# Stationary tokens for the mixer's output projection, turned back by VectorE and DMA, and the first two MLP blocks side by side

## The chip, the cores and the metric

The program runs on one core of a Trainium2 chip. The metric is device time in microseconds (us), the median of the runs. Engines in the profile: PE is TensorE (PEld its weight loads), DVE is VectorE, ACT is ScalarE, POOL is GpSimd, SP is SyncE; a name with q (SPq, ACTq) is that engine's sequencer, where it issues transfers.

## The reference, cut to what matters

One layer on 16 meta tokens and 256 tokens of width 2048, all in float32:

```python
h = h + hybrid_mixer(rmsnorm(h, norm_mix_g), ...)
h = h + squared_relu_mlp(rmsnorm(h, norm_mlp_g), w_ff1, w_ff2)
return rmsnorm(h, final_norm_g)[:, N_META:]

# the end of hybrid_mixer
y = sigmoid(gate_fox) * (o_fox @ w_o_fox) + sigmoid(gate_gla) * (o_gla @ w_o_gla)
return y @ w_out                               # 256 x 2048 times 2048 x 2048

def squared_relu_mlp(xn, w1, w2):              # 2048 -> 8192 -> 2048
    return jnp.square(jax.nn.relu(xn @ w1)) @ w2
```

The part ahead of `y` (projections, forgetting attention, gated linear attention) is left as it was.

## The kernel before, in words

**Products.** Each float32 operand is held as two fp32r parts, high and low, and a product is three matmuls: high by high, high by low, low by high. All weights stream once from HBM in the order of `stream()`, in loads of 512 KB (`raw`, five buffers, issued by SyncE in order). ScalarE copies the high part into a buffer `w` (L133, L177) and VectorE subtracts to get the low part (L134, L178). There are five buffers `w` of one 128x1024 tile pair each, so ScalarE can be five tiles ahead of TensorE and no more.

**Two forms.** `gemm2` keeps a weight tile stationary and streams the tokens (L191: 512 columns, both parts of 256 tokens; L192: 256 columns). Its result has features on partitions, as the residual stream `h` has, 128 output features at a time. `token_rows` keeps 128 tokens stationary and streams 512 weight columns (L224 to L226, twice for 256 tokens). Its result has tokens on partitions, 512 features at a time, and must be turned. A block below is 512 output features; its 16 contraction steps come in four quarters, each one call of `wide_weights` with two tiles `w`.

**A turn.** `turn` transposes 32x32 squares on VectorE (L237), sends the tile to DRAM in four transfers (L244, `there<-turn`) and fetches it back (L248, `turn<-there`), all issued by ScalarE. The list `behind` sets when: each call of `wide_weights` or `next_weights` counts the entries down, and an entry falls due behind the copy of the call's last tile. Slots 5, 6 and 7 are the send, the fetch and the use (`then`).

**Order of the work around the change.** `columns(b)` makes blocks 1, 2 and 3 of `y` in token form and turns them; block 0 is then made by `gemm2` in two pairs of features (`j0` 0 and 2). `y` is split in two parts (L282, L283). The output projection is 16 times `gemm2` over `y`; each result is added to `h`, scaled by the MLP's norm gain into the two parts of `x2`, and its squares are summed in `acc2`. The MLP runs in four groups `g` of 2048 hidden features: ff1 as token blocks (`hidden`: ReLU times `r2` and square on ScalarE, turn, two parts of `a`), then ff2 (`gathered`), which in groups 0 to 2 adds up in token form. In group 0 `norm2` runs inside the first block: four matmuls over `acc2` (L1017), then the root `r2` on VectorE. `spread` (L1024, L1027) sends `r2` through DRAM and broadcasts it into `r2b` on SyncE's queue, between the weight loads. The last group makes two ff1 blocks in token form and the features 8 to 15 with `gemm2`, and its ff2 with `gemm2`. At the end `finish` scales by the last norm and stores.

Tile's scheduler sets each engine's order from a model of the timeline; each engine then works through its order, and a wait holds what stands behind it on that engine.

Of the kernel before, what the change touches and what calls it, by code (L numbers as in the profile page):

```python
# [16 lines left out]
P = 128  # L17
D = 2048
KT = D // P
# [20 lines left out]
def stream():  # L40
# [12 lines left out]
    for j in range(2):  # L53
        s += [("in", O_GF + 128 * j, 0), ("in", O_GG + 128 * j, 0)]
    s += [("in", O_GF + 128 * 2, 0)]
    for b in range(1, 4):
        s += [("in", o + 128 * j, 0) for o in (O_GF, O_GG) for j in range(4 * b, 4 * b + 4)]
        s += [("fox", 128 * j, 0) for j in range(4 * b, 4 * b + 4, 2)]
        s += [("gla", 128 * j, 0) for j in range(4 * b, 4 * b + 4)]
    for j in (0, 2):  # L60
        if j:
            s += [("in", o, 0) for o in (O_GG + 128 * 2, O_GF + 128 * 3, O_GG + 128 * 3)]
        s += [("fox", 128 * j, 0)]
        s += [("gla", 128 * j, 0), ("gla", 128 * (j + 1), 0)]
# [8 lines left out]
def trunk(ctx: ExitStack, tc: tile.TileContext, hT, w_small, w_all, consts, w_alpha2, out):  # L73
# [141 lines left out]
    def token_rows(x, n, between=None, nk=KT, **kw):  # L215

        pts = [[bank(px, "pt") for _ in range(2)] for _ in range(n)]
        for i, q in [(i, q) for i in range(n) for q in range(nk // 4 - 1)] + [(i, nk // 4 - 1) for i in range(n)]:
            w = wide_weights(chunk[0] + 4 * i, q, **kw)
            for k in range(4 * q, 4 * q + 4):  # L220
                hi, lo = w(k)
                for t, ps in enumerate(pts[i]):
                    xh, xl = (x[:, k, o, P * t : P * t + P] for o in range(2))
                    nc.tensor.matmul(steps(ps), xh, steps(hi), start=(k == 0), stop=False)  # L224
                    nc.tensor.matmul(steps(ps), xh, steps(lo), start=False, stop=False)  # L225
                    nc.tensor.matmul(steps(ps), xl, steps(hi), start=False, stop=(k == nk - 1))  # L226
                if between and k == 9:
                    between()
# [4 lines left out]
    def turn(rows, then, both, into=None):  # L233
# [13 lines left out]
        behind.append([5, away])  # L247
        behind.append([6, lambda: nc.scalar.dma_start(back, there)])  # L248
        behind.append([7, lambda: then(back.rearrange("p (c t j r) -> p j t c r", c=4, t=2, r=32))])
# [747 lines left out]
    for j in range(KT):  # L997
        add_residual(j, gemm2(next_weights(), y))
        nc.scalar.activation(x2[:, j, 0, :], ht[:, j, :], AF.Identity, scale=gain(1, j))
        nc.vector.scalar_tensor_tensor(x2[:, j, 1, :], ht[:, j, :], gain(1, j),  # L1000
                                       x2[:, j, 0, :].bitcast(F32), op0=ALU.mult, op1=ALU.subtract)
        square_sum(j, acc2)
# [4 lines left out]
    nc.gpsimd.memset(unit.bitcast(F32), 1.0)  # L1007

# [27 lines left out]
    def turn_tile():  # L1036
        return gat.tile([P, KT * P], F32, tag="o", name=nm("turn"))

    def hidden(a, b, pt):
# [8 lines left out]
        turn([lambda t=t: part(t) for t in range(2)], lambda back: turned_parts(a, b, back), turn_tile())  # L1048
# [3 lines left out]
    def gathered(g, b, pt):  # L1052
# [10 lines left out]
        def add(back):  # L1063
            for j in range(4 * b, 4 * b + 4):
                r = ht[:, j, :].rearrange("p (t c r) -> p t c r", t=2, r=32)
                nc.gpsimd.tensor_tensor(r, r, back[:, j - 4 * b], op=ALU.add)
# [10 lines left out]
    for g in range(NG):  # L1077
# [3 lines left out]
        for b in range(2 if g == NG - 1 else 4):  # L1081
            hidden(a, b, *token_rows(x2, 1, norm2 if (g, b) == (0, 0) else None))
# [3 lines left out]
    for f in range(8, KT):  # L1086
# [74 lines left out]
    def finish(i):  # L1161
# [92 lines left out]
```

## Time and profile before

| What | Value |
|---|---|
| Median of 3 runs (lowest to highest) | 1529.1 us (1528.81 to 1529.36) |
| The profiled execution: time, span | 1529.71 us, 1528.0 us |
| Mean granted TensorE clock | 0.998 |
| Busy PE, DVE, ACT, POOL | 99%, 63%, 51%, 9% of the span |
| HBM read, written | 300.46 MB, 13.12 MB (205 GB/s over the span) |
| Output projection, first matmul to the MLP's first | 752.41 to 838.99 us |
| ff1 of group 0, first matmul to the first of its ff2 | 838.99 to 924.4 us |
| Landing of a weight load, a send, a fetch (median) | 4.0, 4.4, 5.1 us |
| Landing of `line<-r`, of `r2b<-line` (median) | 8.7, 6.9 us |

A row of the order of time gives start, duration, engine, line, operation, output<-input, shapes and count, and in brackets the idle time of the engine before it with what ended it. A row with a count above one is merged, from the first start to the last end. Waits read: engine and line, what was waited for, total us, times, longest.

### The profile page before, as it was taken

How to read it: one execution, taken by the hardware profiler on the slowest of the kernel's cores; microseconds unless marked ns; L12 is line 12 of the kernel's file. 1: busy time of each engine (PE TensorE's matmuls, PEld its weight loads, DVE VectorE, ACT ScalarE, POOL GpSimd, SP SyncE). 2: the span in 40 equal slices, each digit the busy share in tenths (PEclk: the TensorE clock that was granted, in tenths of full speed). 3: DMA queues.
4: the chain of work that ended last, by engine and by line, in shares of the span. 5: the costliest groups of instructions: out<-in, count | busy, mean ns of one | idle time of the engine just before them, and what ended most of it. 6: DMA issues, size and time to landing. Idle time of an engine off the chain costs nothing.

```text
span 1528.0 us, 22647 instructions
## 1 busy us (share of the span) xinstructions
PE 1516.4 (99%) x8646; PEld 1354.7 (89%) x8646; DVE 969.2 (63%) x1355; ACT 781.9 (51%) x1138; POOL 131.1 (9%) x206
## 2 busy tenths in 40 slices
PE   9999999999999999999999999999999999999997
PEld 8999999999998888888899888888888888888997
DVE  7898858586665454546787565445555455656765
ACT  7766444455555434344556455445544455345663
POOL 5012010121101000000011000000000000220012
PEclk9999999999999999999999999999999999999999
DMA  9545555565555667666566587667775677787652
GB/s 321 172 149 182 178 163 186 161 213 169 170 172 181 201 203 223 212 213 210 198 204 199 173 282 253 200 198 238 243 232 195 219 249 245 235 268 246 205 188 103
DMA packets 215472, 315.07 MB, mean 206 GB/s; under 512 B 12170, under 2 KB 180116, under 8 KB 215236
## 3 DMA queue, kind: packets, MB, share of 16 engines
q1 hardware_dynamic: 199636, 289.76, 58.6%
q10 hardware_dynamic: 15552, 22.75, 4.3%
q8 instruction: 68, 1.11, 0.3%
q0 software_dynamic: 176, 1.12, 0.2%
q14 instruction: 40, 0.33, 0.1%
HBM read 300.46 MB, written 13.12 MB: 205 GB/s over the span
## 4 chain that ended last, share of the span: by engine, by line
PE 95%; DVE 2%; ACT 1%; issue 1%; DMA 0%; SPq 0%; POOL 0%; POOLq 0%; DVEq 0%; ACTq 0%
PE ps L191 17%; PE pt L226 17%; PE pt L225 17%; PE pt L224 17%; PE ps L192 9%; PE psa L196 4%; PE psa L200 4%; PE psa L198 4%; PE ps L455 1%; PE ps L1120 1%; PE ps L457 1%; DVE w L134 1%; PE ps L1102 0%; DMA raw<-w_all_dram 0%; PE pa L653 0%
## 5 line engine op out<-in xcount | busy, mean ns | idle before, releaser
L178 DVE TENSOR_TENSOR w<-raw,w 128x1024 fp32r<-128x1024 f32 x292 | 359.6, 1233 | 342.2 <-ACT w L177 330.0
L177 ACT CAST w<-raw 128x1024 fp32r<-128x1024 f32 x292 | 305.1, 1046 | 368.7 <-PE pt L226 353.5
L134 DVE TENSOR_TENSOR w<-raw,w 128x1024 fp32r<-128x1024 f32 x230 | 282.9, 1230 | 109.9 <-ACT w L133 106.8
L133 ACT CAST w<-raw 128x1024 fp32r<-128x1024 f32 x230 | 240.9, 1049 | 101.9 <-PE ps L192 32.2
L226 PE MATMUL pt<-w,x 128*128 128x512 f32 x640 | 243.2, 380 | 0.0
L225 PE MATMUL pt<-w,x 128*128 128x512 f32 x640 | 243.2, 380 | 0.0
L224 PE MATMUL pt<-w,x 128*128 128x512 f32 x640 | 243.2, 380 | 0.0
L191 PE MATMUL ps<-x,w 128*128 128x512 f32 x671 | 227.4, 383 | 0.0
L192 PE MATMUL ps<-x,w 128*128 128x256 f32 x671 | 184.1, 274 | 0.0
L196 PE MATMUL psa<-x,w 128*128 128x272 f32 x640 | 181.7, 285 | 0.0
L200 PE MATMUL psa<-x,w 128*128 128x272 f32 x640 | 179.7, 282 | 0.0
L198 PE MATMUL psa<-x,w 128*128 128x272 f32 x624 | 175.9, 282 | 0.0
L224 PE MATMUL pt<-w,a 128*128 128x512 f32 x384 | 145.9, 380 | 0.0
L225 PE MATMUL pt<-w,a 128*128 128x512 f32 x384 | 145.9, 380 | 0.0
L226 PE MATMUL pt<-w,a 128*128 128x512 f32 x384 | 145.9, 380 | 0.0
L191 PEld LDWEIGHTS ps<-x,w 128*128 128x128 f32 x671 | 126.0, 188 | 21.4
L226 PEld LDWEIGHTS pt<-w,x 128*128 128x128 f32 x640 | 120.1, 188 | 20.7
L224 PEld LDWEIGHTS pt<-w,x 128*128 128x128 f32 x640 | 120.1, 188 | 20.7
L225 PEld LDWEIGHTS pt<-w,x 128*128 128x128 f32 x640 | 120.1, 188 | 20.6
L192 PEld LDWEIGHTS ps<-x,w 128*128 128x128 f32 x671 | 126.0, 188 | 0.0
L196 PEld LDWEIGHTS psa<-x,w 128*128 128x128 f32 x640 | 120.2, 188 | 0.2
L200 PEld LDWEIGHTS psa<-x,w 128*128 128x128 f32 x640 | 120.2, 188 | 0.1
(343 smaller groups left out, 2179.7 us busy)
## 6 DMA issues: line engine op xcount, KB each, us to landing
raw<-w_all_dram SPq DMA_DIRECT2D x525, 512.0 KB, 4.0
there<-turn ACTq DMA_DIRECT2D x72, 128.0 KB, 4.4
turn<-there ACTq DMA_DIRECT2D x18, 512.0 KB, 5.1
raw<-w_all_dram SPq DMA_DIRECT2D x26, 256.0 KB, 3.4
raw<-w_all_dram SPq DMA_DIRECT2D x8, 384.0 KB, 6.7
h<-hT_dram SPq DMA_DIRECT2D x8, 275.0 KB, 6.7
there<-sg ACTq DMA_DIRECT2D x12, 128.0 KB, 4.5
yf<-there ACTq DMA_DIRECT2D x3, 512.0 KB, 4.1
```

Source lines behind the costliest of these rows:

```text
L133: copied = nc.scalar.copy(hi[:, k, :], r).ins
L134: nc.vector.tensor_tensor(lo[:, k, :], r, hi[:, k, :].bitcast(F32), op=ALU.subtract)
L177: copied = nc.scalar.copy(hi, r).ins
L178: nc.vector.tensor_tensor(lo, r, hi.bitcast(F32), op=ALU.subtract)
L191: nc.tensor.matmul(steps(ps), hi, steps(row(x)), start=first, stop=False)
L192: nc.tensor.matmul(steps(ps[:, 0:NT]), lo, steps(x[:, 0, :]), start=False, stop=last)
L196: nc.tensor.matmul(steps(ps[:, X_LO]), hi, steps(x_lo[:, k]), start=first, stop=False, skip_group_check=True)
L198: nc.tensor.matmul(steps(ps[:, 0:NA]), lo, steps(x_hi[:, k]), start=False, stop=last and hi is None, skip_group_check=True)
L200: nc.tensor.matmul(steps(ps[:, 0:NA]), hi, steps(x_hi[:, k]), start=False, stop=last, skip_group_check=True)
L224: nc.tensor.matmul(steps(ps), xh, steps(hi), start=(k == 0), stop=False)
L225: nc.tensor.matmul(steps(ps), xh, steps(lo), start=False, stop=False)
L226: nc.tensor.matmul(steps(ps), xl, steps(hi), start=False, stop=(k == nk - 1))
```

## The change

The output projection uses `token_rows` over `y`, four blocks, each turned (`mixed`); the residual sum, `x2` and the squares follow behind the turn. `y`'s blocks 0 to 2 are now the ones made in token form, and block 3 the one by `gemm2`, so that the last made is the last read. In group 0 the first two ff1 blocks are one call of `token_rows`: three quarters of the first, three of the second, then the last quarter of each, with `norm2` behind step 13 of the first; both are turned at the same slots. The last group makes a third ff1 block in token form. Two smaller edits: the residual sum behind a turned ff2 block takes two wide operations on GpSimd in place of four, and `finish` joins two stores.

```diff
-    for b in range(1, 4):
+    for b in range(3):
         s += [("in", o + 128 * j, 0) for o in (O_GF, O_GG) for j in range(4 * b, 4 * b + 4)]
...
-                if between and k == 9:
+                if between and (i, k) == (0, 13):
                     between()
...
-    def turn(rows, then, both, into=None):
+    def turn(rows, then, both, into=None, slot=5):
...
-        behind.append([5, away])
-        behind.append([6, lambda: nc.scalar.dma_start(back, there)])
-        behind.append([7, lambda: then(back.rearrange("p (c t j r) -> p j t c r", c=4, t=2, r=32))])
+        behind.append([slot, away])
+        behind.append([slot + 1, lambda: nc.scalar.dma_start(back, there)])
+        behind.append([slot + 2, lambda: then(back.rearrange("p (c t j r) -> p j t c r", c=4, t=2, r=32))])
...
-    for b in range(1, 4):
+    for b in range(3):
         columns(b)
-    for j0 in (0, 2):
-        gates = ahead[0:4] if j0 == 0 else [ahead[4]] + [gate() for _ in range(3)]
+    for j0 in (12, 14):
+        gates = ahead[0:4] if j0 == 12 else [ahead[4]] + [gate() for _ in range(3)]
...
-    y = operand(keep, "y", at=16, tag="s1")
+    y = operand(keep, "y", at=48, tag="s1")
...
-    for j in range(4):
+    for j in range(12, KT):
         split_to(y[:, j, 0, :], y[:, j, 1, :], yf[:, j, :])
...
-    for j in range(KT):
-        add_residual(j, gemm2(next_weights(), y))
-        nc.scalar.activation(x2[:, j, 0, :], ht[:, j, :], AF.Identity, scale=gain(1, j))
-        nc.vector.scalar_tensor_tensor(x2[:, j, 1, :], ht[:, j, :], gain(1, j),
-                                       x2[:, j, 0, :].bitcast(F32), op0=ALU.mult, op1=ALU.subtract)
-        square_sum(j, acc2)
+    def mixed(b, pt):
+        def add(back):
+            for t in range(2):
+                r = ht[:, 4 * b : 4 * b + 4, P * t : P * t + P].rearrange("p j (c r) -> p j c r", r=32)
+                nc.vector.tensor_tensor(r, r, back[:, :, t], op=ALU.add)
+            for j in range(4 * b, 4 * b + 4):
+                nc.scalar.activation(x2[:, j, 0, :], ht[:, j, :], AF.Identity, scale=gain(1, j))
+                nc.vector.scalar_tensor_tensor(x2[:, j, 1, :], ht[:, j, :], gain(1, j),
+                                               x2[:, j, 0, :].bitcast(F32), op0=ALU.mult, op1=ALU.subtract)
+                square_sum(j, acc2)
+        turn([lambda ps=ps: ps for ps in pt], add, turn_tile(), slot=4 if b == 3 else 5)
...
+    for b in range(4):
+        mixed(b, *token_rows(y, 1))
...
         def add(back):
-            for j in range(4 * b, 4 * b + 4):
-                r = ht[:, j, :].rearrange("p (t c r) -> p t c r", t=2, r=32)
-                nc.gpsimd.tensor_tensor(r, r, back[:, j - 4 * b], op=ALU.add)
+            for t in range(2):
+                r = ht[:, 4 * b : 4 * b + 4, P * t : P * t + P].rearrange("p j (c r) -> p j c r", r=32)
+                nc.gpsimd.tensor_tensor(r, r, back[:, :, t], op=ALU.add)
...
-        for b in range(2 if g == NG - 1 else 4):
-            hidden(a, b, *token_rows(x2, 1, norm2 if (g, b) == (0, 0) else None))
+        for b0, n in ((0, 2), (2, 1), (3, 1)) if g == 0 else [(b, 1) for b in range(3 if g == NG - 1 else 4)]:
+            for b, pt in enumerate(token_rows(x2, n, norm2 if n == 2 else None), b0):
+                hidden(a, b, pt, 3 if (g, b) == (NG - 1, 2) else 5)
...
-    for f in range(8, KT):
+    for f in range(12, KT):
         relu2(a, f, gemm2(next_weights(low=True), x2))
...
-                store(nc.sync, j0, 4)
+                if j0 == 0:
+                    store(nc.sync, j0, 4)
                 scale(eng, j0 + 4, 4, r)
-                store(nc.sync, j0 + 4, 4)
+                store(nc.sync, j0 + 4 if j0 == 0 else j0, 4 if j0 == 0 else 8)
```

The change moves instructions at two places that the prediction speaks of. Lines of the changed kernel stand up to two lower than those of the kernel before up to the output projection (L177 is L175, L244 is L242, L248 is L246), and some nine higher in the MLP (L1044 is L1053, L1027 is L1039).

First, ScalarE in ff1 of group 0. Before, behind the copies for the first quarter of the third block, it stands so; `turn_8824` is the first block's turned tile, `u_8970` the second block's rows:

```order
L177 CAST w_8982<-raw_8981 128x1024
L177 CAST w_8987<-raw_8986 128x1024
L244 DMA there_8831<-turn_8824 32x4x256 x4
L177 CAST w_9020<-raw_9019 128x1024
L177 CAST w_9025<-raw_9024 128x1024
L248 DMA turn_8824<-there_8831 128x1024
L1044 ACTIVATE u_8970<-pt_8832,r_8653 128x512
L1044 ACTIVATE u_8970<-pt_8833,r_8653 128x512
L177 CAST w_9055<-raw_9054 128x1024
L1045 ACTIVATE u_8970<-u_8970 128x512 x2
L177 CAST w_9060<-raw_9059 128x1024
L282 CAST a_8660<-turn_8824 128x4x128 x2
```

Now, behind the copies `w_8973` and `w_8978` for the first quarter of the fourth block, it stands so; `turn_8806` and `turn_8815` are the first and the second block's tiles, `u_8961` the third block's rows:

```order
L242 DMA there_8813<-turn_8806 32x4x256 x4
L242 DMA there_8822<-turn_8815 32x4x256 x4
L175 CAST w_9015<-raw_9014 128x1024
L175 CAST w_9020<-raw_9019 128x1024
L246 DMA turn_8806<-there_8813 128x1024
L246 DMA turn_8815<-there_8822 128x1024
L1053 ACTIVATE u_8961<-pt_8823,r_7823 128x512
L1053 ACTIVATE u_8961<-pt_8824,r_7823 128x512
L175 CAST w_9051<-raw_9050 128x1024
L1054 ACTIVATE u_8961<-u_8961 128x512 x2
L175 CAST w_9056<-raw_9055 128x1024
L280 CAST a_8450<-turn_8806 128x4x128 x2
```

Sends, fetches and casts of two tiles stand together where those of one stood; the cast of `turn_8815` is the next row, ahead of the next weight copies. Counted in tiles `w` from the MLP's first (tile 0), `w_8973`, `w_8978`, `w_9015`, `w_9020`, `w_9051` and `w_9056` are tiles 24 to 29.

Second, SyncE's queue around `spread`. Before, `raw_8936` and `raw_8941` are the loads for tiles 14 and 15 of the MLP, `line` holds `r2` in DRAM:

```order
L175 DMA raw_8936<-w_all_dram 128x4x256
L175 DMA raw_8941<-w_all_dram 128x4x256
L1024 DMA line<-r_8653 128x1 x2
L175 DMA raw_8981<-w_all_dram 128x4x256
L1027 DMA r2b<-line 128x64 x4
L175 DMA raw_8986<-w_all_dram 128x4x256
```

Now `raw_8927` and `raw_8932` are the loads for tiles 22 and 23:

```order
L173 DMA raw_8927<-w_all_dram 128x4x256
L173 DMA raw_8932<-w_all_dram 128x4x256
L1036 DMA line<-r_7823 128x1 x2
L1039 DMA r2b<-line 128x64 x3
L173 DMA raw_8972<-w_all_dram 128x4x256
L1039 DMA r2b<-line 128x64
L173 DMA raw_8977<-w_all_dram 128x4x256
```

The store of `r2` and its broadcasts come eight tiles later, and no weight load stands between the store and the first broadcast any more.

More of the change, by code (lines that the diff above doesn't have):

```diff
@@ L1034, in relu2, with hidden @@
         split_to(a[:, f, 0, :], a[:, f, 1, :], s)
-    def turn_tile():
-        return gat.tile([P, KT * P], F32, tag="o", name=nm("turn"))
-    def hidden(a, b, pt):
+    def hidden(a, b, pt, slot):
         u = gat.tile([P, 2, 512], F32, tag="u", name=nm("u"), bufs=1)
@@ L1046, in part @@
             return u[:, t, :]
-        turn([lambda t=t: part(t) for t in range(2)], lambda back: turned_parts(a, b, back), turn_tile())
+        turn([lambda t=t: part(t) for t in range(2)], lambda back: turned_parts(a, b, back), turn_tile(), slot=slot)
     rows = gat.tile([P, 2, D], F32, name="rows", bufs=1)
```

12 lines of the change are left out of this document (6 added, 6 removed).

## The prediction

> **What bounds it now.** I read the page first, its busy table and its chain, then PE's waits after the mixer's attention, then the order of time around the places of the change.
>
> ```profile
> PE 1516.4 (99%) x8646; PEld 1354.7 (89%) x8646; DVE 969.2 (63%) x1355; ACT 781.9 (51%) x1138; POOL 131.1 (9%) x206
> PE 95%; DVE 2%; ACT 1%; issue 1%; DMA 0%; SPq 0%; POOL 0%; POOLq 0%; DVEq 0%; ACTq 0%
> PE ps L192 <- DVE w L134: 0.5, 1, 0.5
> PE pn L1146 <- ACT sq L1127: 0.3, 1, 0.3
> ```
>
> TensorE is the bound: 99% busy, 95% of the chain. From 560 us on it waits 0.8 us that the profile can name, so a term must shorten its stream or open a hole in it. "Busy" overlaps neighbours, so I take pitches, from start to start, at the seam between output projection (L191/L192, stationary weights) and MLP (L224 to L226, stationary tokens).
>
> ```profile
> 757.99 0.38 PE L191 MATMUL ps<-y,w 128*128 128x512 f32 x1
> 838.66 0.38 PE L191 MATMUL ps<-y,w 128*128 128x512 f32 x1
> 838.88 0.27 PE L192 MATMUL ps<-y,w 128*128 128x256 f32 x1
> 838.99 0.38 PE L224 MATMUL pt<-w,x 128*128 128x512 f32 x1
> 839.21 0.38 PE L225 MATMUL pt<-w,x 128*128 128x512 f32 x1
> 847.79 0.38 PE L225 MATMUL pt<-w,x 128*128 128x512 f32 x1
> ```
>
> 757.99 is the projection's 14th contraction step and 838.66 its 256th: 80.67 us over 242 steps is 0.3333 us for one step of 128 output columns. 839.21 to 847.79 is 39 matmuls of 512 columns: 0.2200 us each.
>
> **The change, part by part.** *Stationary tokens.* Four projection blocks and one block of the last ff1 change form. A block of 512 output columns took 64 x 0.3333 = 21.33 us; now it is 96 x 0.2200 = 21.12. Five blocks give 5 x 0.213 = **1.07 us**. Both forms stream the same number of columns; the gain is only that fewer, longer matmuls carry it. The Trainium skill (TensorE: Matmul & The Clock Gate, section Back-to-back issue gap) gives a warm matmul of N columns N / 2.4 + 2.5 ns: 215.7 and 109.2 ns, an estimate of 0.43 us for the five blocks. The rows show 220.0 and 113.3 ns, a larger fixed part, so the trace differs and its 1.07 stands.
>
> *y's order.* Before, the blocks finished last in feature layout are y's steps 0 to 3, and the projection starts on them.
>
> ```profile
> 752.41 0.38 PE L191 MATMUL ps<-y,w 128*128 128x512 f32 x1
> 755.30 0.38 PE L192 MATMUL ps<-y,w 128*128 128x256 f32 x1 [0.50 <-DVE w L134]
> 755.62 0.41 ACT L282 CAST y<-yf 128x256 fp32r<-128x256 f32 x1 [1.63 <-DVE yf L967]
> 756.06 0.43 DVE L283 TENSOR_TENSOR y<-yf,y 128x256 fp32r<-128x256 f32 x1 [0.47 <-ACT y L282]
> 756.54 0.50 PE L191 MATMUL ps<-y,w 128*128 128x512 f32 x1
> ```
>
> From the projection's first matmul to the MLP's first are 838.99 - 752.41 = 86.58 us, where 256 x 0.3333 = 85.33 are work: **1.25 us** is lost, all in these rows. The scheduler starts other outputs early, but y's fourth block is ready only at 756.49. After, these are steps 14 and 15, first read 14 x 6 x 0.22 = 18.5 us into the projection and ready 4.1 us into it. The stall goes whole (between 0 and 1.25 I take 1.25); next late is nothing for 14 us.
>
> *The way back from the projection.* Its rows now need two transposes, four sends, one fetch, the residual sum and the two parts of x2. One such turn of the MLP shows the pace:
>
> ```profile
> L224 PE MATMUL pt<-w,a x384: 380/380/380, 924.4 to 1346.1; 128*128 128x512 f32 x192
> 922.07 0.34 ACTq L248 DMA_DIRECT2D turn<-there  x1
> 923.89 1.35 ACT L1044 ACTIVATE u<-pt,r 128x512 f32<-128x512 f32 x2 [0.94 <-PE pt L226]
> 926.07 1.15 ACT L1045 ACTIVATE u<-u 128x512 f32<-128x512 f32 x2
> 928.89 1.14 ACT L282 CAST a<-turn 128x512 fp32r<-128x512 f32 x2 [0.65 <-DMA turn<-there]
> 927.35 1.30 DVE L237 STREAM_TRANSPOSE turn<-u 128x512 f32<-128x512 f32 x2
> 929.67 1.29 DVE L283 TENSOR_TENSOR a<-turn,a 128x512 fp32r<-128x512 f32 x2
> 841.74 0.96 DVE L1000 SCALAR_TENSOR_TENSOR x<-h,x 128x256 fp32r<-128x256 f32 x1
> ```
>
> Consumer at 924.4, turned data usable at 928.9. By the same slots x2's third block is fetched 4.5 us into the MLP. The adds (1.29), one weight subtraction (1.23) and four scalings (at most 0.96 each) end by 4.5 + 1.3 + 1.2 + 3.8 = 10.8; its steps start at 10.6, 11.9, 13.2 and 14.5, and the first is ready at 8.0. Hidden, with 2.6 us of cover. The fourth block has its slots one earlier and is first read after six quarters (31.7 us), since the two MLP blocks leave their last quarters to the end: hidden. If a cover goes, each us missing costs one. I price them 0.
>
> *norm2 and r2.* Rows of the root and of what SyncE does with it:
>
> ```profile
> 852.19 1.04 PE L1017 MATMUL pn<-unit,parts 128*128 128x512 f32 x4
> 856.99 1.23 DVE L178 TENSOR_TENSOR w<-raw,w 128x1024 fp32r<-128x1024 f32 x1 [0.37 <-ACT w L177]
> 858.13 0.15 DVE L326 SCALAR_TENSOR_TENSOR r<-r2r,r 128x2 f32<-128x2 f32 x1
> 858.66 0.97 SPq L1024 DMA_DIRECT2D line<-r  x2
> 860.88 0.38 SPq L175 DMA_DIRECT2D raw<-w_all_dram  x1
> 867.57 1.74 SPq L1027 DMA_DIRECT2D r2b<-line  x4
> 869.41 28.80 SPq L175 DMA_DIRECT2D raw<-w_all_dram  x14
> 877.27 1.05 ACT L177 CAST w<-raw 128x1024 fp32r<-128x1024 f32 x1 [4.47 <-DMA raw<-w_all_dram]
> 879.26 2.05 ACT L177 CAST w<-raw 128x1024 fp32r<-128x1024 f32 x2 [0.95 <-DMA raw<-w_all_dram]
> ACT w L177 <- PE pt L226: 353.5, 233, 2.5
> ```
>
> The root ends 858.28 - 852.19 = 6.1 us after its first matmul. SyncE's line store follows, and the broadcasts into r2b wait 867.57 - 858.66 = 8.9 us for its landing, with every weight load queued behind them. The next load starts at 869.41 and ScalarE gets it at 877.27, 7.9 us later, the one after that 2.0 us later. Before, five weight buffers hid this.
>
> Call a half two contraction steps of a 512-column block: one buffer, 12 x 0.22 = 2.64 us of PE. ScalarE splits half m when PE leaves half m - 5 (the last row is that wait). Count from the MLP's first matmul, 0.88 us of norm2 included: half m is due at 2.64 m + 0.9. Norm2 now stands behind 13 halves, at 34.3: root 40.4, line 40.8, broadcasts 49.7, three of them (1.74 / 4 each) to 51.0, then the load of half 24. Splitting (1.05) and subtracting (1.23) give 51.0 + 7.9 + 2.3 = 61.2, due 64.2. Hidden by 3.0 us, but the queue runs 5.2 us late (half 24's buffer is free at 53.7). The third MLP block needs a bank that the first frees at 40.4 + 1.35 = 41.8, due 43.1: hidden.
>
> *Two MLP blocks side by side.* Both now turn at once; before has this with the ff2 of group 2, where GpSimd takes the data, not ScalarE and VectorE:
>
> ```profile
> 1317.92 4.68 ACTq L244 DMA_DIRECT2D there<-turn  x8
> 1322.69 1.04 ACT L177 CAST w<-raw 128x1024 fp32r<-128x1024 f32 x1 [3.74 <-DMA there<-turn]
> 1323.27 0.34 ACTq L248 DMA_DIRECT2D turn<-there  x1
> 1326.98 0.34 ACTq L248 DMA_DIRECT2D turn<-there  x1
> 1332.63 5.57 POOL L1066 TENSOR_TENSOR h<-h,turn 128x256 f32<-128x256 f32 x4 [0.72 <-DMA turn<-there]
> ```
>
> Eight sends hold ScalarE 1322.69 - 1317.92 = 4.8 us; the second fetch issues 1326.98 - 1317.92 = 9.1 us after the first send, when the second tile's sends have landed, and its own data come 1332.63 - 1326.98 = 5.65 us later. In before all this fell into a slack time of ScalarE. Now it meets the late load queue. Half 25 arrives at 60.9 and the sends go with it. Half 26 is split at 66.7 and subtracted at 68.0 (due 69.5). After half 27 ScalarE stands until 70.0 for the second fetch. Two ReLUs of the third block (1.35) follow, then half 28, done at 74.1 (due 74.8), the squares (1.15) and half 29, done at 76.3 (due 77.4). The casts of both turned tiles (2 x 1.14, the second tile there at 70.0 + 5.65 = 75.7) end at 77.3 and half 30 is split at 78.3. But VectorE has four subtractions and two transposes in front of that half's subtraction (to 79.9), so its low part is there at 81.1, and PE reads it at 80.3: **0.8 us lost**, once, since half 31 is ready at 82.3. On this stretch each us of delay costs one. Bounds: 0, and with both landings a quarter longer (2.3 and 1.4 us) 0.8 + 3.7 = 4.5. I take 0.8, from the rows as they are.
>
> *The rest.* In the last group, block 2 is turned with slot 3: usable 2.5 x 5.33 = 13.3 us after it, read at 21.3 + 8 x 0.33 = 24.0: 0. GpSimd's wider adds are off the chain: 0.
>
> ```profile
> 1517.32 2.34 POOL L1170 TENSOR_TENSOR o<-h,r_half 128x512 f32<-128x512 f32 x2 [0.43 <-DVE r_half L1155]
> 1518.07 6.24 SPq L1173 DMA_DIRECT2D out_dram<-o  x6
> ```
>
> The joined store still leaves when GpSimd ends at 1519.66, 3 us ahead of the last stores: 0, between -0.3 and +0.3.
>
> **The sum.** The profiled execution took 1529.71 us (span 1528.0 and 1.7 around it): 1529.71 - 1.07 - 1.25 + 0.8 = 1528.2. The median of the runs is 0.6 below the profiled one, so 1529.1 - 1.5 = **1527.6 us**. A measurement of this kernel tells about 0.2% (3.1 us) from no change; this lies within it, between 1526.0 and 1532.2.
>
> **Rivals.** *No stall.* If line or loads land a us sooner than in before's rows, half 30 is in time: 1529.1 - 2.3 = 1526.8. For it: single turns left no hole. Against: nowhere in before do a blocked load queue and a double turn meet.
>
> *ScalarE held by the two turns: slower.* Place: group 0, halves 26 to 30. The eight sends run beside the weight loads that catch up, and ScalarE waits in order for the second tile. If the second fetch issues not 9.1 but 18 us after the first send, the hole is 0.8 + 8.9 = 9.7 us: 1526.8 + 9.7 = 1536.5. Against 1529.1 it decides the sign once the hole passes 2.3 us (issue at 10.6), and measurably from 5.4 us (issue at 13.7). For it: DMA was behind in 869 to 880, three loads in 10.9 us. Against: the sends in 1317.92 to 1326.98 held no weight load up. The Trainium skill (DMA: Bandwidth & Descriptors, section Issuing engines are not separate DMA queues) has transfers of both issuers interleave on the same 16 DMA engines, which speaks for this rival; no row of before shows that overlap at its worst.
>
> *Faster than the sum.* No stall and another 0.8 us, from the tail or a stage not named here: 1525.9. PE's rows offer no such hole.
>
> **How the numbers follow.** Forecast (a hole up to 2.3 us, 1526.9 to 1529.1) 0.47; no stall 0.24; a hole of 2.3 to 5.4 us (up to 1532.2) 0.07; slower rival 0.13; faster 0.09. Same is 0.47 + 0.24 + 0.07 = 0.78. The range runs from 1526.0 to 1530.5: all of the first two, some two thirds of the next (0.05) and half of the fast case (0.04), 0.80 together; the slow rival stays outside.
>
> **What would show it.** PE's seam: projection in 84.5 us without a hole at its start; L191's successors at 0.22 pitch. In group 0, SyncE's broadcasts about 50 us after the MLP's first matmul, ScalarE waiting for raw and then for the sent tiles, and a PE gap below 1 us near 80 us (half 30). A gap earlier, at x2's third block or at the first half behind the broadcasts, or one above 2.3 us, would make the sum wrong; so would a projection pitch other than 0.22.

## The result, and the profile after

The changed kernel takes **1535.5 us** (median of 20 runs, 1526.65 to 1547.53); the kernel before took 1528.82 us on the same chip (20 runs, 1528.27 to 1530.75). The ratio is 1.0038, with a 95% interval of 1.0026 to 1.0051. The forecast of 1527.6 us and the range up to 1530.5 were wrong. The runs fall into groups: four at 1526.7 to 1527.9 us, where the forecast's sum without a stall lies (1526.8), fourteen at 1532 to 1537 and two at 1546 and 1548. The profiled execution took 1535.48 us, span 1533.8.

From the page after, the busy line:

```profile
PE 1523.7 (99%) x8486; PEld 1348.2 (88%) x8486; DVE 959.4 (63%) x1327; ACT 777.2 (51%) x1120; POOL 129.6 (8%) x198
```

TensorE still bounds it and is busier by 7.3 us. Its list of waits after names nothing behind the mixer but the last norm:

```profile
PE pn L1156 <- ACT sq L1137: 0.3, 1, 0.3
```

So no hole explains the loss. The seam, in order of time, is what the prediction wanted:

```profile
751.34 0.38 PE L222 MATMUL pt<-w,y 128*128 128x512 f32 x1
835.81 0.38 PE L222 MATMUL pt<-w,x 128*128 128x512 f32 x1
```

The projection takes 835.81 - 751.34 = 84.47 us, 384 x 0.2200, where it took 86.58: 2.1 us are won there, stall and form together. The loss comes later. The stretches of the profile, of after (first fence) and of the kernel before (second), with start and end, length, PE's busy time and matmuls, granted clock, share of DMA and GB/s:

```profile
850.00:900.00 50.00, 50.00 (x229) 1.00 0.69 210
1020.00:1200.00 180.00, 180.00 (x807) 1.00 0.68 220
```

```profile
850.00:900.00 50.00, 50.00 (x229) 1.00 0.69 210
1020.00:1200.00 180.00, 180.00 (x819) 1.00 0.69 222
```

From 850 to 900 us the two do the same number of matmuls in the same time. From 1020 us on, at the same granted clock of 1.00 and with PE busy throughout, after does 807 in 180 us where before did 819: 180 / 807 = 0.2230 us against 0.2198. **The matmuls follow one another at a longer pitch**, with no idle time between. Here it begins: in order of time, matmuls and then the loads ahead of them. PEld loads what a matmul keeps stationary, here the tokens `x`; L223 is the matmul that streams the low part of `w`.

```profile
915.69 0.38 PE L224 MATMUL pt<-w,x 128*128 128x512 f32 x1
915.91 0.39 PE L222 MATMUL pt<-w,x 128*128 128x512 f32 x1
916.14 0.39 PE L223 MATMUL pt<-w,x 128*128 128x512 f32 x1
916.37 0.39 PE L224 MATMUL pt<-w,x 128*128 128x512 f32 x1
```

```profile
915.69 0.19 PEld L222 LDWEIGHTS pt<-w,x 128*128 128x128 f32 x1
915.97 0.19 PEld L223 LDWEIGHTS pt<-w,x 128*128 128x128 f32 x1
```

Each load starts within 0.01 us of the matmul ahead of it, except L223's at 915.97, which is 0.06 us late. The rows' steps go from 0.22 to 0.23, and they do not go back to 0.220. Far behind:

```profile
999.73 0.39 PE L222 MATMUL pt<-w,a 128*128 128x512 f32 x1
1000.62 0.39 PE L223 MATMUL pt<-w,a 128*128 128x512 f32 x1
```

That is 0.89 us for four steps, which alternate between about 222 and 225 ns; over 96 matmuls from 934.74 to 956.18 us the average is 21.44 / 96 = 0.2233, 223.3 ns. From 916 us to the end of the token blocks at 1414 us are 498 / 0.2233 = 2,230 matmuls, 7.4 us at 3.3 ns more each. Behind them the form with stationary weights is long as well, 0.340 us a step (five steps from 1414.45 to 1416.15) for 0.3333: from its first matmul (1414.45) to the last of all (1525.85) the trace has 111.4 us, where the kernel with r2 on GpSimd (below) has 109.9 (1407.18 to 1517.05), 1.5 us more. That makes 8.9 us, against 2.1 won.

What is late at 915.97 is the low part of tile 30, the place that the prediction named (half 30). SyncE, ScalarE and VectorE in order of time:

```profile
876.60 0.97 SPq L1036 DMA_DIRECT2D line<-r  x2
885.08 1.27 SPq L1039 DMA_DIRECT2D r2b<-line  x3
894.08 8.88 ACTq L242 DMA_DIRECT2D there<-turn  x8
903.06 1.05 ACT L175 CAST w<-raw 128x1024 fp32r<-128x1024 f32 x1 [7.96 <-PE pt L224]
905.30 0.40 ACTq L246 DMA_DIRECT2D turn<-there  x1
911.11 2.49 DVE L281 TENSOR_TENSOR a<-turn,a 128x512 fp32r<-128x512 f32 x4
913.52 1.30 DVE L235 STREAM_TRANSPOSE turn<-u 128x512 f32<-128x512 f32 x2
914.74 2.32 DVE L176 TENSOR_TENSOR w<-raw,w 128x1024 fp32r<-128x1024 f32 x2
```

The first of the two subtractions at 914.74 ends at 915.92; the load, due at 915.91, starts 0.05 us behind that end.

Ten microseconds earlier the low part of tile 26 had been late too. Its load and the matmuls around it:

```profile
905.42 0.19 PEld L223 LDWEIGHTS pt<-w,x 128*128 128x128 f32 x1
905.33 0.39 PE L222 MATMUL pt<-w,x 128*128 128x512 f32 x1
905.57 0.38 PE L223 MATMUL pt<-w,x 128*128 128x512 f32 x1
```

This load came 0.09 us after the matmul ahead of it, later than tile 30's. Yet from 905.57 to 915.69 there are 46 steps in 10.12 us, 0.2200 each: the short pitch came back. So being late is not by itself enough.

### The profile page after: what moved, and what is told of

The parts are those of the page before. It is cut to its first block, busy times and chain, and to the rows that moved or that the text cites. A ratio compares the mean times of both kernels' runs of the same rounds, so it can differ in the third digit from the quotient of the medians.

```text
span 1533.8 us, 22288 instructions
## 1 busy us (share of the span) xinstructions
PE 1523.7 (99%) x8486; PEld 1348.2 (88%) x8486; DVE 959.4 (63%) x1327; ACT 777.2 (51%) x1120; POOL 129.6 (8%) x198
## 4 chain that ended last, share of the span: by engine, by line
PE 96%; DVE 2%; ACT 1%; issue 1%; POOL 0%; POOLq 0%; DVEq 0%; ACTq 0%
PE pt L222 19%; PE pt L224 19%; PE pt L223 19%; PE ps L189 12%; PE ps L190 6%; PE psa L194 4%; PE psa L198 4%; PE psa L196 4%; PE ps L453 1%; PE ps L455 1%; PE ps L1130 1%; DVE w L132 1%; PE ps L1112 0%; PE pa L651 0%; PE po L709 0%
## 5 line engine op out<-in xcount | busy, mean ns | idle before, releaser
L175 ACT CAST w<-raw 128x1024 fp32r<-128x1024 f32 x332 | 346.6, 1046 | 420.1 <-PE pt L224 400.3
L223 PE MATMUL pt<-w,x 128*128 128x512 f32 x672 | 256.7, 382 | 0.0
L224 PE MATMUL pt<-w,x 128*128 128x512 f32 x672 | 256.6, 382 | 0.0
L222 PE MATMUL pt<-w,x 128*128 128x512 f32 x672 | 256.5, 382 | 0.0
L189 PE MATMUL ps<-x,w 128*128 128x512 f32 x607 | 206.4, 384 | 0.0
L190 PE MATMUL ps<-x,w 128*128 128x256 f32 x607 | 166.7, 275 | 0.0
L223 PE MATMUL pt<-w,a 128*128 128x512 f32 x384 | 147.3, 384 | 0.0
L223 PEld LDWEIGHTS pt<-w,x 128*128 128x128 f32 x672 | 126.0, 188 | 23.1
L222 PEld LDWEIGHTS pt<-w,x 128*128 128x128 f32 x672 | 126.0, 188 | 23.1
L224 PEld LDWEIGHTS pt<-w,x 128*128 128x128 f32 x672 | 126.0, 188 | 23.0
L189 PEld LDWEIGHTS ps<-x,w 128*128 128x128 f32 x607 | 113.9, 188 | 19.7
L194 PEld LDWEIGHTS psa<-x,w 128*128 128x128 f32 x640 | 120.2, 188 | 0.2
L198 PEld LDWEIGHTS psa<-x,w 128*128 128x128 f32 x640 | 120.1, 188 | 0.1
L196 PEld LDWEIGHTS psa<-x,w 128*128 128x128 f32 x624 | 117.4, 188 | 0.0
```

The source lines that it names most:

```text
L175: copied = nc.scalar.copy(hi, r).ins
L189: nc.tensor.matmul(steps(ps), hi, steps(row(x)), start=first, stop=False)
L190: nc.tensor.matmul(steps(ps[:, 0:NT]), lo, steps(x[:, 0, :]), start=False, stop=last)
L194: nc.tensor.matmul(steps(ps[:, X_LO]), hi, steps(x_lo[:, k]), start=first, stop=False, skip_group_check=True)
L196: nc.tensor.matmul(steps(ps[:, 0:NA]), lo, steps(x_hi[:, k]), start=False, stop=last and hi is None, skip_group_check=True)
L198: nc.tensor.matmul(steps(ps[:, 0:NA]), hi, steps(x_hi[:, k]), start=False, stop=last, skip_group_check=True)
```

## The experiments

**Two ways to undo the meeting.** The theory from here on: the late load at tile 30, however small, set the longer pitch, and it comes from two things at once, SyncE's queue held by r2 and two turns that meet. The first edit puts the second block's turn two calls later, the second takes r2 off SyncE.

```diff
-                hidden(a, b, pt, 3 if (g, b) == (NG - 1, 2) else 5)
+                hidden(a, b, pt, 3 if (g, b) == (NG - 1, 2) else 7 if (g, b) == (0, 1) else 5)
```

> The changed kernel, but the second block of group 0 is turned two calls later (slots 7, 8, 9 in place of 5, 6, 7), so that its sends, fetch and casts do not fall together with the first block's. Theory S (a near miss sets a slower pitch): in the profile of the changed kernel tile 30 of the MLP comes 0.07 us late, and from there to the end the pitch of a 512-column matmul is 223.3 ns in place of 220.0; without the meeting of the two turns tile 30 is some 3 us early, the pitch stays 220 and every run takes 1526.8 +- 0.5 us, with a spread like before's. Rival C (the slower pitch is a state of the chip that has nothing to do with the turns, or comes of the larger DMA traffic): about two thirds of the runs still take 1535 us and the profile may show 223 ns.

It took 1535.67 us (1527.62 to 1542.09; ratio 1.0030, 1.0012 to 1.0049), five of the 12 runs at 1527.6 to 1529.8 and the others at 1534 or more: no cure. Yet the pitch is 0.220 at tile 30 and stays so until 932 us, where `a`'s second block now comes too late. In order of time:

```profile
932.06 0.39 PE L224 MATMUL pt<-w,a 128*128 128x512 f32 x1
933.00 0.50 PE L222 MATMUL pt<-w,a 128*128 128x512 f32 x1 [0.55 <-ACT a L280]
933.34 0.39 PE L223 MATMUL pt<-w,a 128*128 128x512 f32 x1
934.10 0.48 PE L224 MATMUL pt<-w,a 128*128 128x512 f32 x1 [0.38 <-DVE a L281]
```

Two real waits, 1.3 us together (steps of 0.94 and 0.76 where 0.22 was due), and behind them 223.3 ns again. The edit had taken one late operand away and made another.

```diff
-            nc.sync.dma_start(line[:, P * t : P * t + P].rearrange("o p -> p o"), r2[:, t : t + 1])
+            nc.gpsimd.dma_start(line[:, P * t : P * t + P].rearrange("o p -> p o"), r2[:, t : t + 1])
...
-            nc.sync.dma_start(r2b[:, cols], line[:, cols].to_broadcast([P, 64]))
+            nc.gpsimd.dma_start(r2b[:, cols], line[:, cols].to_broadcast([P, 64]))
```

> The changed kernel, but the store of r2 and its broadcasts are issued by GpSimd, so that no weight load waits behind them; the two turns still meet. Theory S, with the lateness made of two parts: the load queue is on time, the sends start some 5 us earlier and tile 30 is early by about 3 us: 220 ns throughout, 1526.8 +- 0.5 us in every run. If the meeting of the turns alone makes the near miss: 1535 us in most runs, as the changed kernel. Rival C: 1535 us in about two thirds of the runs.

**1527.04 us** (1526.3 to 1528.05, 11 runs; ratio 0.9982, 0.9974 to 0.9991). SyncE's weight loads now run through the place where they had been held, VectorE is 2.3 us earlier at tile 30 (912.43 for 914.74), and from 1020 to 1200 us there are 820 matmuls again. In order of time:

```profile
879.98 12.64 SPq L173 DMA_DIRECT2D raw<-w_all_dram  x6
912.43 4.59 DVE L176 TENSOR_TENSOR w<-raw,w 128x1024 fp32r<-128x1024 f32 x4
```

This is the kernel that the forecast without a stall (1526.8) described, and it beats both kernels, the one before by 0.2%.

**Is it the wait, or what stands around it?** A probe makes TensorE wait in a quiet place: a matmul, a ScalarE copy of its result, a matmul on the copy, inserted between two matmuls of a token block of group 1. First in the changed kernel, then in the kernel with r2 on GpSimd, and there once more in the last group.

```diff
+    def ask():
...
+        mm = nc.tensor.matmul(steps(ps), parts[:, 0:P], steps(unit), start=True, stop=True)
...
+    def answer(cols):
+        nc.scalar.copy(parts[:, P : P + cols], asked.pop()[:, 0:cols])
...
+        mm = nc.tensor.matmul(steps(ps), parts[:, P : 2 * P], steps(unit), start=True, stop=True)
...
+            probes.extend([None, (0, 384)])
```

> The changed kernel, with one forced wait of PE some 95 us behind tile 30 (in the second quarter of group 1's first block): a matmul, a ScalarE copy of its result, and a matmul that reads the copy, with nothing between them, so that PE stands about 1 us. It adds two matmuls (0.44 us). Theory S with a pitch that a real wait sets back: 223 ns from tile 30 to the wait (some 1.4 us lost), 220 behind it: 1526.8 + 1.4 + 1.4 = 1529.6 us where tile 30 is late. Theory S with a pitch that stays: 1535.5 + 1.4 = 1537 us. Rival C: 1537 us in two thirds of the runs, with no tie to the wait.

1533.82 us (6 runs, 1531.94 to 1536.72), not slower than the changed kernel. In its profiled execution tile 30 was in time, the pitch was 0.220 up to the probe at 1012.67 us, 223.3 ns from it to the end of the token blocks, and 0.3333 us per step again in the second projection. So here the probe's wait began the long pitch, and the change of form ended it. Whether a wait can set a long pitch back this run does not tell, since the pitch ahead of the probe was short.

> The changed kernel with r2 on GpSimd (1527.04 us, pitch 220.0 ns to the end) plus one forced wait of TensorE in group 1: a matmul, a ScalarE copy of 384 columns, a matmul on its result, put between two matmuls of the second quarter (the profile of the same probe in another kernel: 0.74 us and 0.10 us of excess and two matmuls of 0.22 us, 1.3 us in all). Theory (a wait in a stream of tokens can leave TensorE on a longer pitch until the next thing that disturbs it): modes at 1528.3 us (pitch 220.0), about 1534.2 us (223.3 ns over the 1,790 matmuls to the end of the token stages, 5.9 us) and up to 1535.7 us (also behind them); median 1532 to 1535. Rival (a wait costs itself and no more): 1528.3 us in every run. Rival (the slow pitch belongs to r2's broadcasts or to the two turns, not to a wait): 1528.3 us too.

**1534.15 us** in ten runs of 1533.91 to 1535.02, for 1528.3 if a wait cost itself only. In order of time:

```profile
1010.25 2.14 PE L246 MATMUL pt<-w,x 128*128 128x512 f32 x9
1013.18 0.49 PE L225 MATMUL gp<-unit,parts 128*128 128x512 f32 x1 [0.57 <-ACT parts L223]
1013.51 4.68 PE L246 MATMUL pt<-w,x 128*128 128x512 f32 x20
```

Nine matmuls ahead: (2.14 - 0.38) / 8 = 0.220. Twenty behind: (4.68 - 0.39) / 19 = 0.226, and then 807 matmuls from 1020 to 1200 us, the number of the changed kernel. The probe with its wait of 0.57 us cost 7.1 us against the kernel without it, of which 1.3 are the wait and the two added matmuls.

> The same forced wait, but in the last group: about 250 token matmuls and the second projection's 650 behind it instead of 1,790 and 650. Theory: the same pitches cost less there, 250 x 3.3 ns = 0.8 us to the end of the token stages and 1.5 us at most behind them: modes at 1528.3, 1529.1 and 1530.6 us, median 1528.3 to 1530.6. Rival (a forced wait costs a fixed sum wherever it stands, 1.3 us or the 7 us of the earlier probe): 1528.3 us or about 1534 us, as the other kernel of this call.

1529.39 us (1528.48 to 1530.3): the same probe costs 2.4 us in the last group, 1.1 beyond itself, and behind it the pitch is 223.3 ns up to the change of form. The cost goes with the matmuls left, not with the wait.

**Many waits.** Two ladders put 32 probes each into group 1 of the kernel before, one for each quarter: one with different distances and copies, one that asks for no matmul between question and answer, with the copy's width raised in steps of 16, twice.

> The kernel before, with 32 such round trips from PE to ScalarE and back, one in each quarter of group 1; between question and answer stand 6 to 0 of the block's own matmuls, so that the answer is early, just in time, or late by up to a us. It adds 64 matmuls (14 us) and the waits (some 10 us): about 1553 us with the pitch at 220 throughout. Theory S: behind one of the answers that are late by a tenth of a us or two the pitch goes to 223 and stays for at least some quarters; whether a longer wait sets it back shows at the answers with nothing between (about 1 us). If the pitch stays slow to the end, up to 9 us more. Rival C: the pitch does not change at any of the answers.

1564.1 us (one run), above the 1553 of a pitch of 220 ns throughout. Only some probes made TensorE wait. The first four did not, and the pitch stayed at 220.0 ns. Then it was 228.3 ns behind a wait of 1.46 us (from start to start, beyond one step) and behind the next three probes, late by 0.01 us at most, 223.3 behind the next wait, and 220.0 again behind an answer that was only 0.01 us late.

> The kernel before plus 32 forced waits in group 1, one in each quarter of a block, 24 matmuls apart: TensorE is drained each time, and the ScalarE copy that it waits for is 128 to 368 columns wide in steps of 16, the series run twice. Theory (each wait sets the pitch anew, by the moment at which TensorE starts again): the pitch behind a wait is one of several values, 220.0 among them, also right behind a slow one, and changes from wait to wait. If it goes by the length of the wait alone, the two series give the same pitches for the same widths; if by something finer, they differ. Rival (the first wait brings 223.3 ns, which stays to the end or until the form changes): one step at the first wait and 223.3 behind all. The waits themselves cost 32 x (0.75 to 1.3 us) = 24 to 42 us: 1553 to 1571 us before the pitch.

1572.37 us (one run), above the sum. The edit did not drain TensorE each time: in the trace 17 of the 32 probes have 2 to 22 of the block's own matmuls between question and answer, and 9 made TensorE wait for nothing. Five of its waits, each the probe's answer and the matmuls behind it:

```profile
1045.06 0.48 PE L227 MATMUL gp<-unit,parts 128*128 128x512 f32 x1 [0.48 <-ACT parts L225]
1045.38 4.18 PE L248 MATMUL pt<-w,x 128*128 128x512 f32 x18
1107.40 0.49 PE L227 MATMUL gp<-unit,parts 128*128 128x512 f32 x1 [0.15 <-ACT parts L225]
1107.73 5.59 PE L248 MATMUL pt<-w,x 128*128 128x512 f32 x24
1121.01 0.50 PE L227 MATMUL gp<-unit,parts 128*128 128x512 f32 x1 [2.17 <-ACT parts L225]
1121.35 4.26 PE L248 MATMUL pt<-w,a 128*128 128x512 f32 x18
1146.78 0.48 PE L227 MATMUL gp<-unit,parts 128*128 128x512 f32 x1 [0.46 <-ACT parts L225]
1147.10 4.34 PE L248 MATMUL pt<-w,a 128*128 128x512 f32 x19
1210.90 0.49 PE L227 MATMUL gp<-unit,parts 128*128 128x512 f32 x1 [0.16 <-ACT parts L225]
1211.22 5.44 PE L248 MATMUL pt<-w,a 128*128 128x512 f32 x24
```

Less the last matmul (0.38 to 0.39) and divided by the steps, the pitches are 0.223, 0.226 (which settles at 223.3 ns), 0.228, 0.220 and 0.220. The short pitch comes back behind some waits, so the long one is not a state that only grows. Waits of 0.46 and 0.48 us are followed by 0.220 and 0.223. The rows at 1107.40 and 1210.90 are the same copy of 352 columns in the two series, each with two of the block's matmuls between, and their waits of 0.15 and 0.16 us are followed by 0.226 and 0.220. Neither the wait's length, to 0.02 us, nor the copy's width tells which pitch comes. What does is not settled.

**Is r2's other queue a gain by itself?** The kernel before with the same edit as the cure:

> The kernel before, with only the line store and the four broadcasts of r2 issued by GpSimd instead of SyncE. Theory (GpSimd's issue helps the changed kernel only because it frees SyncE's weight loads there): TensorE has no wait and no slow pitch to lose behind r2 in the kernel before, so the time stays, 1528.3 to 1529.8 us, ratio 0.9995 to 1.0005. Rival (r2's other queue is a gain of its own, and the changed kernel's own edits bring nothing): about 1527.0 us, ratio 0.9985. The two projections that follow from the theory's other half, 1.07 us of token form and 1.25 us of stall, are then what the changed kernel with r2 on GpSimd has over the kernel before.

1530.42 us (1529.86 to 1540.37) against 1529.1; ratio 1.0016, 0.9996 to 1.0036. No gain. The kernel before has runs with a loss too: in this call four of its 29 lie at 1538 to 1539.4 us, beside three of this kernel's 12 at 1539 to 1540.4, and in a later call two of 15; no profile caught one of them. The edited kernel's profiled execution (1531.56 us) shows the old stall of `y` doing what the probe did, in the form with stationary weights. L191 just ahead of the stall, and two rows three steps apart far behind it:

```profile
753.10 0.38 PE L191 MATMUL ps<-y,w 128*128 128x512 f32 x1
753.44 0.39 PE L191 MATMUL ps<-y,w 128*128 128x512 f32 x1
...
799.86 0.39 PE L191 MATMUL ps<-y,w 128*128 128x512 f32 x1
800.88 0.39 PE L191 MATMUL ps<-y,w 128*128 128x512 f32 x1
```

A step ahead takes the usual 0.3333 (0.34 in rows of two digits); behind, three steps take 1.02 us, 0.340 each, up to the end of the projection: 240 x 0.0067 = 1.6 us on top of the stall.

**y's order alone**, in the kernel before, with the stream of weights to match:

```diff
-    for b in range(1, 4):
+    for b in range(3):
         columns(b)
-    for j0 in (0, 2):
+    for j0 in (12, 14):
...
-    for j in range(4):
+    for j in range(12, KT):
         split_to(y[:, j, 0, :], y[:, j, 1, :], yf[:, j, :])
```

> The kernel before with one part of the change alone: the other order of y's blocks (0, 1, 2 by turns, 12 to 15 last). The projection and the MLP stay as before. Theory (term 2): the stall of 1.25 us at the start of the output projection goes, since the last ready blocks are read last, and with it the one wait that can set another pitch there: 1529.1 - 1.25 = 1527.85 us, 1527.4 to 1528.3, and no run near 1539. Rival (y's last blocks then come late in the first gemm instead, since a gemm of 16 steps reaches block 12 after 4 us): 1528.8 us or more. Against the changed kernel with r2 on GpSimd (1527.04 us) it is then the 1.07 us of the token form that are missing: 0.8 us between the two.

1528.76 us (1528.4 to 1529.35), ratio 0.9991 (0.9983 to 1.0000); 1527.85 was expected. The stall is gone, no matmul of the projection waits, and still, from first to last:

```profile
751.68 0.38 PE L189 MATMUL ps<-y,w 128*128 128x512 f32 x1
837.88 0.40 PE L222 MATMUL pt<-w,x 128*128 128x512 f32 x1
```

86.20 us, where 256 x 0.3333 = 85.33 are work: 0.9 us went into a longer pitch, 0.3367 a step, that begins within a microsecond of the first row, at no wait that the profile names.

**The smallest cure.** One call later instead of two, r2 left on SyncE:

```diff
-                hidden(a, b, pt, 3 if (g, b) == (NG - 1, 2) else 5)
+                hidden(a, b, pt, 3 if (g, b) == (NG - 1, 2) else 6 if (g, b) == (0, 1) else 5)
```

> The changed kernel with the turn of the first pair's second block put one call later (slot 6 instead of 5; slot 7 kept pitch 220.0 at the place of the miss, but brought a's second block 0.9 us too late 16 us further on). r2 stays on SyncE. Theory (the miss at tile 30 needs both SyncE's wait behind r2 and the two turns meeting on ScalarE and VectorE): one call is 5.3 us, enough to part the turns and still early for a's second block, so no matmul is late, the pitch stays 220.0 and the time is 1526.8 us, 1526.3 to 1528.0, like the kernel with r2 on GpSimd. Rival (r2's wait alone makes the loads late): 1534 to 1536 us as the changed kernel. Rival (any later turn brings a's block late): real waits of 0.3 to 1 us near 932 us and again a longer pitch, 1528 to 1540 us.

**1526.87 us** (one run of 11 at 1535.07, the others at 1526.28 to 1527.29; ratio 0.9985, 0.9975 to 0.9995). Now VectorE reaches tile 30 ahead of the transposes:

```profile
912.81 1.22 DVE L176 TENSOR_TENSOR w<-raw,w 128x1024 fp32r<-128x1024 f32 x1 [1.33 <-ACT w L175]
913.96 1.30 DVE L235 STREAM_TRANSPOSE turn<-u 128x512 f32<-128x512 f32 x2
```

It ends at 914.03, 2 us ahead of its matmul. Tile 26's low part, late in the changed kernel, ends 5.7 us ahead here and 2.8 us ahead with r2 on GpSimd. So undoing either half brings the time down, and the misses at tiles 26 and 30 needed both.

**r2 later.** The store and the broadcasts moved a group back in the program:

```diff
-        if g == 1:
+        if g == 2:
             spread()
```

> The changed kernel with r2's line store and broadcasts still on SyncE, but issued a group later (group 2's place instead of group 1's), where the blocks run one by one and no two turns meet; r2 is first used behind the token stages. Theory (not the queue but the meeting of the two makes the miss): SyncE still waits some 7 to 12 us for the line to land, the weight buffers behind it hold the loads off, but no matmul waits: pitch 220.0, 1526.8 us (1526.3 to 1528). Rival (12 us of SyncE's wait are too much for the ring of weight buffers anywhere): a late weight tile about 85 to 170 us further on, a longer pitch from there on, 1529 to 1535 us.

1536.78 us (1527.15 to 1548.41). The edit did not do what it says: the scheduler left r2's store and broadcasts where they were in SyncE's order, and the broadcasts start at 885 us in both. It is a second sample of the changed kernel on another chip, with the same spread, and tells nothing about the rival. Its profiled execution (1534.18 us) is all the same worth a look, at tile 26:

```profile
905.64 0.39 PE L222 MATMUL pt<-w,x 128*128 128x512 f32 x1
905.66 0.19 PEld L223 LDWEIGHTS pt<-w,x 128*128 128x128 f32 x1
```

The load is 0.02 us late, and here the longer pitch begins at it and stays, with 807 matmuls from 1020 to 1200 us. In the first profile of the changed kernel 0.09 us at the same tile left the pitch at 220.0, and 0.06 us at tile 30 did not. How late an operand is does not tell which pitch follows.

**Both cures, and a second tight place.** Slot 6 and r2 on GpSimd together:

> The changed kernel with both cures: r2's store and broadcasts on GpSimd, and the second block's turn one call later. Theory (either cure alone already takes away the late load, so that a second adds nothing but margin): 1526.9 us, 1526.2 to 1527.6, ratio to the kernel before 0.9980 to 0.9988, and no run in the 1534 to 1548 us where a longer pitch would put it. Rival (the two edits take from each other, since GpSimd's queue and the later turn now fall together): a late load again and 1530 us or more. Rival (each cure removed a loss of its own): 0.5 us or more below either, 1526.3 us or less.

1527.03 us (1526.65 to 1535.5; ratio 0.9979, 0.9966 to 0.9991). No gain over one cure, and one run of 12 with a longer pitch, the profiled one. It begins at x2's third block. VectorE, PE and PEld:

```profile
846.02 2.23 DVE L1006 SCALAR_TENSOR_TENSOR x<-h,x 128x256 fp32r<-128x256 f32 x3
846.92 0.39 PE L223 MATMUL pt<-w,x 128*128 128x512 f32 x1
847.03 0.19 PEld L224 LDWEIGHTS pt<-w,x 128*128 128x128 f32 x1
```

The first of the three low parts (0.96) ends at 846.98, and its load starts at 847.03, 0.11 us late. With r2 on GpSimd alone, the same operation ended at 845.65, 1.2 us earlier counted from the MLP's first matmul. The last two kernels turn that block one call sooner, with r2 on GpSimd and then with slot 6:

```diff
-        turn([lambda ps=ps: ps for ps in pt], add, turn_tile(), slot=4 if b == 3 else 5)
+        turn([lambda ps=ps: ps for ps in pt], add, turn_tile(), slot=4 if b >= 2 else 5)
```

> The changed kernel with r2 on GpSimd, and the turn of the projection's third block one call earlier (slot 4, as the fourth block has it), so that x2's third block is there 5.3 us sooner. In the profile of the kernel with both cures that block's first low part ended 0.11 us after its matmul was due, in another run of the same program 1.3 us before. Theory (the few runs near 1535 us that are left with either cure come from this place): 1527.0 us as before, 1526.2 to 1528.0 in every run, none above 1530. Rival (they come from elsewhere, or from nothing in the program): about one run in twelve near 1535 again. Rival (two turns of the projection now meet on ScalarE, and x2's fourth block or the second comes late): 1528 us or more at the median.

1527.21 us, 1526.4 to 1528.05 in all 11 runs (ratio 0.9986, 0.9977 to 0.9995).

> The same earlier turn of the projection's third block, in the changed kernel with r2 on SyncE and the second MLP block's turn one call later (1526.87 us, one run of 11 at 1535.07). Theory: 1526.9 us, 1526.2 to 1528.0 in every run. Rival (the run at 1535.07 was the first weight loads behind r2, which this leaves as they are): again a run near 1535 among twelve. Rival (the earlier turn meets the one ahead of it): 1528 us or more at the median.

1526.64 us, but two runs of 12 at 1535.3 and 1535.9 (ratio 0.9992, 0.9979 to 1.0005), as the first rival had it. What sets the longer pitch in those two no profile caught; in the profiled execution the low parts of tiles 24 to 31 are all there some 3 us or more ahead of their matmuls. With r2 on GpSimd the longer pitch came in none of 11 runs, one of 12 and none of 11, too few to say that the earlier turn did it.

## Why the prediction was wrong

- **Token form, 1.07 us:** held in the projection, with pitch 0.2200 and 84.47 us for the 84.5 expected. The fifth block, in the last group, ran at the longer pitch in the profiled execution. (The 0.43 us quoted beside it is 0.40 by its own formula; the sum does not use it.)
- **y's stall, 1.25 us:** held in the changed kernel, where form and order together gave the 2.1 us. With the order alone, 0.9 us of it went into a longer pitch.
- **norm2, r2, the queue:** the times from the MLP's first matmul (835.81) were close. Line store 40.8 expected, 40.8 in the rows; broadcasts 49.7 and 49.3. The second fetch came at 69.5 for 70.0, but by luck: the loads behind r2 were there 2.6 us sooner than priced (half 24 is split at 56.3 for 58.9), and the eight sends held ScalarE 8.9 us (894.08 to 902.96) for the 4.8 of the profile of before.
- **Half 26, "subtracted at 68.0 (due 69.5)":** too early. Behind the longer sends its low part was there at 69.6, so that its load came 0.09 us late where 1.5 us of cover were counted.
- **x2's third block, "hidden, with 2.6 us of cover":** too much. Its first low part was priced ready at 8.0. The rows have 7.5 in after, 9.6 in the kernel with r2 on GpSimd and 10.8 in the one with both cures, where it was due by then.
- **Half 30, "0.8 us lost, once": the step that failed.** The place was right, and its low part was there at 80.1 instead of 81.1, due at 80.1 (the prediction's 80.3 is the matmul; its load is due a step earlier). The load came 0.06 us late, its matmul 0.01. But the price was taken as the hole's length, by the sentence that each microsecond of delay costs one. The runs show a second price: a late operand can put TensorE on another pitch, which it keeps over thousands of matmuls. A load 0.06 us late was followed by 8.9 us of loss. Why this one was and tile 26's was not stays open.
- **Rivals:** "no stall" (1526.8) is where four of the 20 runs are, and the cured kernels. "ScalarE held by the two turns" gave 1536.5 us, near the time measured, but by a hole of 9.7 us that does not exist; its number was right by accident. Its condition came in part: the second fetch was issued 11.2 us after the first send (9.1 in the sum, 18 in the rival), but the sends began 2.6 us sooner. No rival had a change of pitch in it, and the profile of before showed none behind its one stall, y's: the steps there went back to 0.3333.

## What to carry to other kernels

Where one engine is 99% busy, compare its pitch between two profiles before looking for holes: the count of matmuls in equal stretches, at equal granted clock, shows a 1.5% loss that no list of waits does. An operand that arrives at the moment when it is due may cost far more than its delay; give the operands of such a stream two microseconds or more of cover, as the kernels near 1527 us have at tiles 26 and 30, and beware of small transfers on the queue that carries the weight loads together with two turns due in the same call. When the runs of a kernel fall into groups, look for a near miss, and remember that a profile of one group says nothing of the other.

## What the runs showed of the hardware

A stream of 512-column matmuls with one weight load each ran at one of several steady pitches, at the same granted clock (0.997 to 0.999 over each execution): 220.0 ns, 223.3 (alternating 222 and 225), and 228.3 (about 222, 230, 229 and 232 in turn). The form with stationary weights ran at 0.3333, 0.3367 or 0.340 us a step. Nearly every change stood where an operand came late, by 0.01 to 2 us, or where the form of the products changed; the one in the kernel with y's order alone stood at no wait. Behind it the pitch kept its value, for some 500 us in the changed kernel. Not every late operand changes it: 0.09 us at tile 26 left it, 0.02 us at the same tile of the same order of work set 223.3. The three groups of the changed kernel's runs fit these values: 8.9 us at 223.3, and at 228.3 about 8.3 / 3.3 x 7.4 = 19 us for the token matmuls, an estimate, where two runs lie 18 and 20 us above the middle of the fast ones; no profile caught one of these two. Why a wait leads to one pitch or another, and what in TensorE makes them, no run here shows.
